# A hybrid decoder block on one Trainium2 core: the gate's row written in 128-byte pieces, and the two heads' A products untied

## The chip, the cores and the metric

The kernel runs on one core of a Trainium2 chip. The metric is the device time of one execution, in microseconds. Engines are named as in the profile: PE (TensorE's matmuls), PEld (its weight loads), DVE (VectorE), ACT (ScalarE), POOL (GpSimd) and SP (SyncE). All DMAs of the program are issued from SP's queue.

## The reference

A decoder block with two token mixers side by side on one normalised input, for 2048 tokens of width 1024:

```python
mod = einsum('bd,de->be', silu(c), ada_w) + ada_b
shift, scale, gate = split(mod, 3)
h = rmsnorm(x, norm_g) * (1 + scale) + shift
p = h @ w_in                                   # split into the branches' inputs
y_conv = conv_branch(...)                      # GLU, causal depthwise conv of 31, LayerNorm, swish, projection
y_rwkv = rwkv7_branch(...)                     # delta-rule state per head of 64, group norm, projection
m = sigmoid(g_conv) * y_conv + sigmoid(g_rwkv) * y_rwkv
out = rmsnorm(x + gate * (m @ w_out), final_g)
```

The RWKV branch runs a recurrence over tokens with one 64 by 64 state per head:

```python
sk = einsum('bhvk,bhk->bhv', state, kk_t)
state = state * w_t - sk * b_t + v_t * k_t     # outer products
o_t = einsum('bhvk,bhk->bhv', state, r_t)
```

The change touches two places of this: how `gate`, a vector of 1024 numbers, gets to DRAM, and the order in which one kind of small matrix product inside the RWKV branch is issued.

## The kernel before

The tokens are cut into 4 blocks of 512. In its first phase, up to about 2410 us, the kernel makes for each block all input projections, the convolution and the RWKV recurrence. In its second it makes the output projections, the final sum and the norm. All large products are made with operands split into a high and a low part, three matmuls for each (`mm3k`, line 207, tile `ps_main`). The weights' high and low parts are made once, kept in DRAM and loaded again for each later block by `load_w` (lines 183 and 184), as `w_hi` and `w_lo`, 512 KB each.

The RWKV branch works in chunks of 64 tokens, 8 chunks for a block. The 16 heads form 8 pairs, and two pairs form a group: 4 groups for each block. `pair` (line 457) prepares one pair of heads, both on the 128 partitions, head 0 on the first 64 and head 1 on the last 64. Its A products (line 535) multiply the tiles `BK` and `KR` of each chunk and head: matmuls with a contraction of 64 rows and 128 columns moving. They are made in two halves (`c4`) of 4 chunks. In each half, head 0 writes one PSUM tile of tag "aux" and head 1 another; VectorE then empties them with a mask into `Asb` (line 545). The tag has three buffers (`PAB`), which the pair's other small products use too, so the second half finds one buffer free, and needs another that VectorE has to empty first. Before the change, `tc.issue_after` ties the order: head 1's product of the first chunk is queued behind head 0's, and all products of the other three chunks of that half are queued behind head 1's first product. These ties are edges of order on TensorE alone, not waits.

A group's As blocks go to DRAM and back around a triangular inversion on POOL: `dA<-As` (line 619, 16 transfers of 16 KB), `La<-dA`, the loop of lines 631 to 636, `dT<-TT`, and `As<-dT` (line 646, 16 transfers of 16 KB).

The order on each engine comes from a planner: the program is traced in the order of the source, and when the context closes, a simulation of the engines takes the instructions by priority as their inputs and buffers come free in it. The engines then execute the order that it wrote, each its own queue in order. So while one group's small products wait, matmuls of line 207 for the convolution and the gates are put between them, and an edited order in one place can move others.

`gate` is made in block 1. `gate_cols` (line 870) is called after each of its four groups and makes two 128-number columns of the gate: it multiplies rows of `ada_w` by the activated `c` and sums them along the row on VectorE (line 878). After the last group, lines 881 to 883 finish the 128 by 8 tile `hgate_col`, and line 884 writes it to the DRAM vector `grow_d`, column by column. In block 2, `ogate` (line 149) reads parts of that vector, spread over all partitions (line 156), and multiplies the output weights by them. The write is issued at 1222.5 us of the span, the first read at 1395.4 us.

Of the kernel before, what the change touches and what calls it, by code (L numbers as in the profile page):

```python
# [9 lines left out]
F32 = mybir.dt.float32  # L10
# [8 lines left out]
P = 128  # L19
D = 1024  # L20
KT = D // P
# [61 lines left out]
def hybrid_block(ctx: ExitStack, tc: tile.TileContext, x, vecs, convk, w2a2, final_g, ada, w_in, w_co, w_ro, w_o, crow, out,  # L83
                 seq=2048, groups=(0, 1, 2, 3), phase2=True, dbg=None):
    nc = tc.nc
# [4 lines left out]
    cst = ctx.enter_context(tc.tile_pool(name="cst", bufs=1))  # L90
# [14 lines left out]
    grow_d = dp.tile([D], F32, name="grow_d", tag="grow_d")  # L105
# [7 lines left out]
    def vc(name, j=None):  # L113
        o, w = VOFF[name]
        return v[:, o:o + w] if j is None else v[:, o + j:o + j + 1]

    g_col = cst.tile([P, KT], F32, name="g_col")
    hgate_col = cst.tile([P, KT], F32, name="hgate_col")
    ghalf = cst.tile([P, 2, KT], F32, name="ghalf")
    shift_col = cst.tile([P, KT], F32, name="shift_col")  # L120
    ones = cst.tile([P, P], F32, name="ones")
# [12 lines left out]
    def flat(ap):  # L134
        return ap.rearrange("p a b -> p (a b)")
# [130 lines left out]
    nc.sync.dma_start(v, vecs)  # L266
    ab = vc("ada_b")
    hlg = cst.tile([P, KT], F32, name="hlg")
    hlb = cst.tile([P, 24], F32, name="hlb")[:, :KT]
    nc.vector.tensor_scalar(out=hlg, in0=vc("conv_ln_g"), scalar1=0.5, scalar2=None, op0=ALU.mult)  # L270
    nc.vector.tensor_scalar(out=hlb, in0=vc("conv_ln_b"), scalar1=0.5, scalar2=None, op0=ALU.mult)

# [57 lines left out]
    def hx(name):  # L330
        return xp.tile([P, TB], F32, name=name, tag="hx")
# [125 lines left out]
    def pair(b, q_, pr, h, lora, uv, Asb, rn, res):  # L457
# [30 lines left out]
        KR = l3.tile([P, NCH // 2, 4 * CH], F32, name="KR", tag="KR", bufs=KRB)  # L488
        BK = l3.tile([P, NCH // 2, 4 * CH], F32, name="BK", tag="BK", bufs=BKB)
# [14 lines left out]
        for c in range(NCH):  # L504
            nc.tensor.matmul(pss[prow(c % 2), c // 2, :], sq[:, c * CH:c * CH + CH], hones, start=True, stop=True,
                             skip_group_check=True)
# [20 lines left out]

        for c4 in range(NCH // 4):
            pA = [pa.tile([P, 2, 256], F32, name="aux", tag="aux") for _ in range(2)]

            def aprod(c, hh):
                cc, e = (c4 * 4 + c) // 2, c % 2
                es = slice(e * 128, e * 128 + 128)
                hs = slice(64 * hh, 64 * hh + 64)
                return nc.tensor.matmul(pA[hh][:, c // 2, es], BK[hs, cc, es], KR[hs, cc, es],  # L535
                                        start=(c == 0), stop=(c == 3), skip_group_check=True)

            with tc.issue_after(aprod(0, 0).ins):
                second = aprod(0, 1)
            with tc.issue_after(second.ins):  # L540
                for c in range(1, 4):
                    for hh in range(2):
                        aprod(c, hh)
            for hh in range(2):
                nc.vector.tensor_tensor(  # L545
                    out=Asb[:, hh, c4 * 4:c4 * 4 + 4, :].rearrange("p (a e) n -> p a (e n)", e=2),
                    in0=pA[hh], in1=flat(maskA).unsqueeze(1).broadcast_to([P, 2, 256]), op=ALU.mult)
# [24 lines left out]
        for c4 in range(NCH // 4):  # L572
            pt = pa.tile([P, 4, P], F32, name="aux", tag="aux")
            for c in range(4):
                cc, e = (c4 * 4 + c) // 2, c % 2
# [5 lines left out]
    def group(b, g, h, lora, fill):  # L581
        uv = l3.tile([P, NCH, 2, P], F32, name="uv", tag="uv", bufs=2)
        As = [l3.tile([P, 2, NCH, P], F32, name="As", tag="As", bufs=ASB) for _ in range(2)]
        R = [{}, {}]
        rn = lt.tile([P, 2, NCH // 2, 2], F32, name="rn", tag="rn")
        pairs = [pair(b, q, 2 * g + q, h, lora, uv, As[q], rn, R[q]) for q in range(2)]
        for i, q in enumerate(ORD):
            next(pairs[q])
# [281 lines left out]
    def gate_cols(g):  # L870
        for half in range(2):
            hs = slice(half * TB, half * TB + TB)
            sr = hx("sr")
            nc.sync.dma_start(sr, srow_d[hs].unsqueeze(0).broadcast_to([P, TB]))
            for k in (2 * g, 2 * g + 1):
                at = hx("gt")
                nc.sync.dma_start(at, ada[16 + k][:, hs])
                nc.vector.scalar_tensor_tensor(out=at, in0=at, scalar=1.0, in1=sr, op0=ALU.mult, op1=ALU.mult,
                                               accum_out=ghalf[:, half, k:k + 1])
        if g == 3:  # L880
            nc.vector.tensor_tensor(out=hgate_col, in0=ghalf[:, 0], in1=ghalf[:, 1], op=ALU.add)
            nc.vector.tensor_tensor(out=hgate_col, in0=hgate_col, in1=ab[:, 16:24], op=ALU.add)
            nc.vector.tensor_scalar(out=hgate_col, in0=hgate_col, scalar1=0.5, scalar2=None, op0=ALU.mult)
            nc.sync.dma_start(grow_d.rearrange("(n p) -> p n", p=P), hgate_col)

    mod = lt.tile([P, 16], F32, name="mod", tag="rn")

# [10 lines left out]
    for b in range(NB):  # L898
        h = hprep(b) if b else hprep0(x0, ada_steps())
        lora = lora_split(h)  # L900
        for g in groups:
# [32 lines left out]
            if b == 1:  # L934
                gate_cols(g)
# [136 lines left out]
    for b in range(NB):  # L1072
# [7 lines left out]
        for tt in range(NTT):  # L1080
            xh = []
            for half in range(2):
                n = 2 * tt + half
# [97 lines left out]
```

## Time and profile before

| | |
|---|---|
| median of 3 runs | 3003.95 us (2998.5 to 3004.62) |
| the profiled execution's own time | 3006.85 us |
| its span from the first instruction to the last | 3005.1 us |
| mean granted TensorE clock | 0.973 |
| instructions | 64777 |
| moved by DMA | 699.26 MB, mean 233 GB/s |

Times in the views are microseconds from the start of the span, durations of single instructions in ns where a view says so. In a timeline, a row gives start, length, engine, line, operation, output and inputs, and how many instructions were merged; in brackets stands how long the engine was idle before it, and what ended that. An fp32 matmul is recorded as two instructions, so 512 A products are 1024 records. A view by stretches gives for each engine its busy time and count, then the granted clock, the share of the DMA engines that was busy, and GB/s. In the DMA table the last number is the median from issue to landing.

### The profile page before, as it was taken

The numbers are of one execution on the slowest core, as the hardware profiler recorded it, in microseconds if no ns is written. First come the engines' busy times: TensorE is split into PE (matmuls) and PEld (weight loads), VectorE is DVE, ScalarE is ACT, GpSimd is POOL, SyncE is SP. The second block draws the span as 40 slices with busy tenths as digits, with TensorE's granted clock in tenths as the row PEclk, the third lists the DMA queues.
The fourth block names the chain that finished last, engine by engine and source line by source line (L and its number), as shares of the span: only waits on it lengthen the run. The fifth ranks groups of instructions, "written<-read, shape, count | busy, mean of one in ns | idle before, by whom it ended". The sixth has DMA issues, their size and how long they took to land.

```text
span 3005.1 us, 64777 instructions
## 1 busy us (share of the span) xinstructions
PE 2821.2 (94%) x25672; PEld 2649.1 (88%) x25672; DVE 2053.8 (68%) x3896; ACT 936.6 (31%) x1759; POOL 1251.2 (42%) x1786
## 2 busy tenths in 40 slices
PE   6889898999999999799999999999999998899998
PEld 5889798999899998799989988999989978688988
DVE  6687778787767676767676758776789634776433
ACT  4433334342324242323231413232333212333201
POOL 3555455535343435143434354626467104555000
PEclk9999999999999999899999999999999999999999
DMA  8666758664768588747575777655547678889674
GB/s 308 221 225 223 238 209 288 228 226 150 263 195 285 160 264 287 215 143 235 159 241 160 247 236 263 209 185 177 198 149 274 218 260 311 330 297 339 241 283 167
DMA packets 368674, 699.26 MB, mean 233 GB/s; under 512 B 136241, under 2 KB 154993, under 8 KB 368370
## 3 DMA queue, kind: packets, MB, share of 16 engines
q1 hardware_dynamic: 368370, 695.10, 68.5%
q8 instruction: 203, 3.33, 0.4%
q14 instruction: 101, 0.83, 0.1%
HBM read 506.14 MB, written 187.70 MB: 231 GB/s over the span
## 4 chain that ended last, share of the span: by engine, by line
PE 41%; DMA 14%; DVE 13%; POOL 11%; issue 4%; SPq 3%; ACT 2%; POOLq 0%; DVEq 0%; ACTq 0%
PE ps_main L207 30%; POOL TT L635 3%; POOL itmp L633 3%; DVE acc L782 3%; DMA w_st<-w_ro_t 2%; DMA w_gr<-grow_d 2%; DMA La<-dA 2%; PE aux L535 1%; PE xo L697 1%; DMA xt<-x_in 1%; DMA dT<-TT 1%; PE pout L1102 1%; PE pout L1103 1%; PE pout L1101 1%; PE xo L692 1%
## 5 line engine op out<-in xcount | busy, mean ns | idle before, releaser
L207 PE MATMUL ps_main<-h_hi,w_lo 128*128 128x256 f32 x4608 | 952.3, 285 | 23.8 <-DMA w_lo<-kl_in 14.9
L207 PE MATMUL ps_main<-h_hi,w_hi 128*128 128x256 f32 x4608 | 951.3, 285 | 14.2 <-ACT w_hi L190 5.4
L207 PE MATMUL ps_main<-h_lo,w_hi 128*128 128x256 f32 x4608 | 951.6, 285 | 0.3 <-DVE h_lo L364 0.3
L207 PEld LDWEIGHTS ps_main<-h_hi,w_lo 128*128 128x128 f32 x4608 | 719.2, 192 | 32.9 <-DMA w_lo<-kl_in 15.6
L207 PEld LDWEIGHTS ps_main<-h_hi,w_hi 128*128 128x128 f32 x4608 | 720.2, 192 | 26.4 <-ACT w_hi L190 6.3
L207 PEld LDWEIGHTS ps_main<-h_lo,w_hi 128*128 128x128 f32 x4608 | 719.5, 192 | 7.8 <-DVE h_lo L364 0.5
L782 DVE SCALAR_TENSOR_TENSOR acc<-u,ck,acc 128x512 f32<-128x512 f32 x928 | 697.9, 752 | 19.9
L633 POOL TENSOR_TENSOR itmp<-La,TT 128x126 f32<-128x126 f32 (+22 forms) x496 | 181.6, 366 | 158.6 <-DMA La<-dA 123.5
L635 POOL TENSOR_TENSOR TT<-TT,itmp 128x126 f32<-128x126 f32 (+22 forms) x496 | 189.7, 382 | 36.8
L689 ACT ACTIVATE Se<-S,pe 128x128 f32<-128x128 f32 x256 | 89.2, 396 | 258.9 <-DVE S L707 258.7
L192 POOL TENSOR_TENSOR w_lo<-w_st,w_hi 128x1024 fp32r<-128x1024 f32 x47 | 113.6, 2417 | 121.2 <-ACT w_hi L190 120.9
L707 DVE TENSOR_TENSOR S<-xo,Se 64x128 f32<-64x128 f32 x256 | 73.4, 287 | 101.3 <-PE xo L703 98.3
L190 ACT CAST w_hi<-w_st 128x1024 fp32r<-128x1024 f32 x71 | 74.6, 1051 | 178.8 <-DMA w_st<-w_in_t 133.1
L699 DVE TENSOR_TENSOR uv<-xo,rn 64x256 f32<-64x256 f32 x128 | 53.8, 420 | 94.8 <-PE xo L697 93.6
L694 DVE TENSOR_TENSOR XO<-xo,XO 128x256 f32<-128x256 f32 x128 | 53.8, 420 | 81.9 <-PE xo L692 67.7
L570 POOL TENSOR_TENSOR BK<-BK,pe 128x1024 f32<-128x1024 f32 x32 | 62.1, 1941 | 113.7 <-PE aux L535 82.3
L794 ACT ACTIVATE th<-ps_main 128x512 f32<-128x512 f32 x64 | 38.2, 597 | 196.7 <-PE ps_main L207 162.9
L692 PE MATMUL xo<-S,KR 128*128 128x128 f32 x512 | 84.7, 289 | 15.7 <-DVE S L707 15.6
L545 DVE TENSOR_TENSOR As<-aux,maskA 128x512 f32<-128x512 f32 x128 | 83.0, 685 | 24.0 <-PE aux L535 23.1
L535 PE MATMUL aux<-KR,BK 64*128 64x128 f32 x1024 | 95.1, 303 | 4.1 <-POOL KR L523 2.5
L697 PE MATMUL xo<-XO,As 64*64 64x64 f32 x1024 | 90.7, 228 | 8.4 <-DVE XO L694 8.2
L697 PEld LDWEIGHTS xo<-XO,As 64*64 64x64 f32 x1024 | 71.2, 136 | 29.3 <-DVE XO L694 10.8
(301 smaller groups left out, 5290.4 us busy)
## 6 DMA issues: line engine op xcount, KB each, us to landing
w_hi<-kh_in SPq DMA_DIRECT2D x219, 512.0 KB, 5.4
w_lo<-kl_in SPq DMA_DIRECT2D x219, 512.0 KB, 4.1
w_st<-w_in_t SPq DMA_DIRECT2D x73, 512.0 KB, 4.7
kh_in<-w_hi SPq DMA_DIRECT2D x71, 512.0 KB, 2.9
kl_in<-w_lo SPq DMA_DIRECT2D x71, 512.0 KB, 3.7
w_hi<-kh_ro SPq DMA_DIRECT2D x32, 512.0 KB, 6.3
w_lo<-kl_ro SPq DMA_DIRECT2D x32, 512.0 KB, 5.7
w_hi<-kh_co SPq DMA_DIRECT2D x32, 512.0 KB, 5.9
```

What stands on the lines that cost most here:

```text
L190: nc.scalar.copy(hi, st)
L192: lo_eng.tensor_tensor(out=lo, in0=st, in1=hi.bitcast(F32), op=ALU.subtract)
L207: nc.tensor.matmul(ps[:, qs], ww[:, k, :], aa[k][:, qs], start=(k == 0 and t == 0 and q == 0), stop=(k == KT - 1 and t == 2 and q == ms - ...
L535: return nc.tensor.matmul(pA[hh][:, c // 2, es], BK[hs, cc, es], KR[hs, cc, es], start=(c == 0), stop=(c == 3), skip_group_check=True)
L545: nc.vector.tensor_tensor(out=Asb[:, hh, c4 * 4:c4 * 4 + 4, :].rearrange("p (a e) n -> p a (e n)", e=2), in0=pA[hh], in1=flat(maskA).unsqu ...
L633: nc.gpsimd.tensor_tensor(out=tmp[:, :ni, :nt], in0=La[:, j:j + 1, j + 1:].broadcast_to([P, ni, nt]), in1=TT[:, :ni, j:j + 1].broadcast_to ...
L635: nc.gpsimd.tensor_tensor(out=TT[:, :ni, j + 1:], in0=TT[:, :ni, j + 1:], in1=tmp[:, :ni, :nt], op=ALU.add)
L689: nc.scalar.mul(Se[:, q, :], Sg[:, q, :], R[q]["pe"][:, c:c + 1])
L692: nc.tensor.matmul(xo[:, q, :], R[q]["KR"][:, cc, es], Sg[:, q, :], start=(q == 0), stop=(q == 1), skip_group_check=True)
L697: nc.tensor.matmul(xo[pr_, q, hs], As[q][pr_, hh, c, kcol(e)], XO[pr_, c, q, hs], start=(q == 0 and hh == 0), stop=(q == 1 and hh == 1), s ...
L707: nc.vector.tensor_tensor(out=Sg[hs, :, hs], in0=xo[hs, 2:4, hs], in1=Se[hs, :, hs], op=ALU.add)
L782: nc.vector.scalar_tensor_tensor(out=acc if i + 1 < HALO else yj, in0=u[:, i:i + TB], scalar=ck[:, j, i:i + 1], in1=acc, op0=ALU.mult, op1 ...
```

## The change

Three edits. The gate's tile `hgate_col` becomes a part of a larger tile of two 32-column planes, cleared at the start. After the column is finished, VectorE transposes the first plane into the second in blocks of 32 by 32, so that the numbers that lie one behind the other in DRAM lie along a partition in runs of 32. Four DMAs then write 8 runs of 128 bytes each, in place of one DMA that writes 1024 single numbers. The padding of another small tile, `hlb`, goes from 24 to 32 columns. And the A products lose their ties: the same products are traced in the same order, chunk by chunk and head by head, without the edges.

```diff
-    hgate_col = cst.tile([P, KT], F32, name="hgate_col")
+    g32 = cst.tile([P, 2, 32], F32, name="g32")
+    nc.vector.memset(g32, 0.0)
+    hgate_col = g32[:, 0, 0:KT]
...
-    hlb = cst.tile([P, 24], F32, name="hlb")[:, :KT]
+    hlb = cst.tile([P, 32], F32, name="hlb")[:, :KT]
...
             pA = [pa.tile([P, 2, 256], F32, name="aux", tag="aux") for _ in range(2)]
-
-            def aprod(c, hh):
+            for c in range(4):
                 cc, e = (c4 * 4 + c) // 2, c % 2
                 es = slice(e * 128, e * 128 + 128)
-                hs = slice(64 * hh, 64 * hh + 64)
-                return nc.tensor.matmul(pA[hh][:, c // 2, es], BK[hs, cc, es], KR[hs, cc, es],
-                                        start=(c == 0), stop=(c == 3), skip_group_check=True)
-
-            with tc.issue_after(aprod(0, 0).ins):
-                second = aprod(0, 1)
-            with tc.issue_after(second.ins):
-                for c in range(1, 4):
-                    for hh in range(2):
-                        aprod(c, hh)
+                for hh in range(2):
+                    hs = slice(64 * hh, 64 * hh + 64)
+                    nc.tensor.matmul(pA[hh][:, c // 2, es], BK[hs, cc, es], KR[hs, cc, es],
+                                     start=(c == 0), stop=(c == 3), skip_group_check=True)
...
             nc.vector.tensor_scalar(out=hgate_col, in0=hgate_col, scalar1=0.5, scalar2=None, op0=ALU.mult)
-            nc.sync.dma_start(grow_d.rearrange("(n p) -> p n", p=P), hgate_col)
+            nc.vector.transpose(g32[:, 1, :], g32[:, 0, :])
+            for i in range(4):
+                nc.sync.dma_start(grow_d.rearrange("(n i t) -> i n t", i=4, t=32)[i], g32[32 * i:32 * i + KT, 1, :])
```

## The prediction

> **What bounds the kernel now.** I read the page first: the busy shares, then the chain that ended last.
>
> ```profile
> PE 2821.2 (94%) x25672; PEld 2649.1 (88%) x25672; DVE 2053.8 (68%) x3896; ACT 936.6 (31%) x1759; POOL 1251.2 (42%) x1786
> ...
> PE 41%; DMA 14%; DVE 13%; POOL 11%; issue 4%; SPq 3%; ACT 2%; POOLq 0%; DVEq 0%; ACTq 0%
> ```
>
> TensorE is occupied for 94% of the span. Its share of the chain is only 41%, so other things do end waits, but each of them briefly. Next I asked for the busy time by stretches: once for the whole mixer phase, 85 to 2410 us, in which all A products lie, and once closely around the gate's row.
>
> ```profile
> core 0: us, PE busy (x) PEld busy (x) DVE busy (x) ACT busy (x) POOL busy (x), PEclk, DMA share, GB/s
> 85.00:2410.00 2325.00, 2206.57 (x21996) 2109.94 (x21995) 1689.89 (x3112) 749.49 (x1379) 1057.52 (x1635) 0.97 0.66 218
> ```
>
> TensorE has work in 2206.57 of 2325 us, 95%, so 118 us are idle. Work added to TensorE here mostly lengthens the kernel.
>
> ```profile
> 1220.00:1224.00 4.00, 4.00 (x36) 3.96 (x35) 3.38 (x11) 0.00 (x0) 0.00 (x0) 1.00 0.30 31
> 1224.00:1228.00 4.00, 0.16 (x2) 0.00 (x0) 4.00 (x11) 0.00 (x0) 0.00 (x0) 0.86 1.49 84
> 1228.00:1232.00 4.00, 0.00 (x0) 0.00 (x0) 0.41 (x1) 0.00 (x0) 0.00 (x0) 0.50 0.49 31
> 1232.00:1236.00 4.00, 0.00 (x0) 0.00 (x0) 0.00 (x0) 0.60 (x1) 0.00 (x0) 0.50 0.61 114
> ```
>
> From 1228 to 1236 no engine has more than a few tenths of a microsecond of work: the program stands still. The timelines of SyncE's queue and of TensorE show what it waits for.
>
> ```profile
> 1212.24 10.16 SPq L646 DMA_DIRECT2D As<-dT  x16
> 1222.49 0.38 SPq L884 DMA_DIRECT2D grow_d<-hgate_col  x1
> 1222.92 0.58 SPq L765 DMA_DIRECT2D ro_d<-th  x1
> 1223.60 0.39 SPq L184 DMA_DIRECT2D w_lo<-kl_in  x1
> ```
> ```profile
> 1223.77 0.39 PE L207 MATMUL ps_main<-h_lo,w_hi 128*128 128x256 f32 x2
> 1236.99 0.79 PE L207 MATMUL ps_main<-h_hi,w_lo 128*128 128x256 f32 x2 [12.83 <-DMA w_lo<-kl_in]
> ```
>
> The gate's row (L884) is issued at 1222.49. The low half of the next weight tile is issued 1.1 us behind it, and TensorE stands for 12.83 us until that lands. The DMA table of the page and the view of line 884 give the two durations to compare.
>
> ```profile
> w_lo<-kl_in SPq DMA_DIRECT2D x219, 512.0 KB, 4.1
> ```
> ```profile
> L884 SPq DMA_DIRECT2D grow_d<-hgate_col x1: 382/382/382, 1222.5 to 1222.5; - x1
> ...
> DMA to landing us min/median/max: 10.9/10.9/10.9
> ```
>
> A transfer like the late one needs 4.1 us at the median. The gate's row carries 4 KB, but as 8 columns by 128 partitions, hence 1024 pieces of 4 bytes, and needs 10.9 us. What is issued behind it inherits that.
>
> **Part 1: the gate's row.** Removed: one transfer of 1024 pieces. Added: a transpose on VectorE, four transfers of 8 pieces of 128 bytes, and a memset at the start. The nearest row for the new transfers is the one that writes As to DRAM, also in runs of 32 floats, 128 bytes (16 KB each, so 128 pieces); for the transpose, line 661.
>
> ```profile
> L619 SPq DMA_DIRECT2D dA<-As x256: 302/430/1792, 96.9 to 2282.1; - x128
> ...
> DMA to landing us min/median/max: 1.4/1.7/7.5
> ```
> ```profile
> L661 DVE STREAM_TRANSPOSE T<-As x128: 255/299/305, 175.8 to 2348.6; 32x128 f32<-32x128 f32 x128
> ```
> ```profile
> 1216.90 0.16 DVE L883 TENSOR_SCALAR hgate_col<-hgate_col 128x8 f32<-128x8 f32 x1
> ```
>
> The transpose costs about 0.3 us after 1217.06. SyncE reaches the row at 1222.49, so 5 us of cover remain; without it, the 0.3 us would fall on SyncE's queue. The wait that the first new transfer has on the transpose is therefore over before SyncE comes to it; behind it in the queue stand the ro_d store and the weights. The memset is of the size of the others at the start:
>
> ```profile
> 0.91 0.17 DVE L122 MEMSET ones<- 128x128 f32 x1 [0.91 <-PEq L1174]
> ...
> 4.92 0.20 DVE L300 COPY maskA<-m 64x64 f32<-64x64 f32 x1 [0.92 <-POOL m L297]
> ```
>
> It disappears in the 0.92 us that VectorE waits there anyway; without that cover it would be 0.17 us. The larger tiles move what is allocated behind them by 256 bytes; no row prices an address, and I count nothing for it.
>
> Three more issues at 0.43 us move the weight's issue from 1223.60 to 1224.9; at the rate of the sixteen issues above (10.16/16 = 0.635) to 1225.5. Its landing then takes 4.1 us, because the queues are nearly empty (31 GB/s in 1220 to 1224), so TensorE resumes at 1229.0 instead of 1236.99: 8.0 us saved. With 3.5 us of landing the saving is 8.6. The other bound is the median of the same transfers in the crowded surroundings:
>
> ```profile
> w_lo<-kl_in SPq DMA_DIRECT2D x8, 512.0 KB, 6.8
> ```
>
> With 6.8 us and the late issue it is 1232.3, a saving of 4.7. I take 7.5, near the empty-queue end. As every engine stands still here, all of it counts. What is late next is the same weight, for about 5 us instead of 12.8, now because sixteen small transfers stand ahead of it on SyncE.
>
> A rule speaks against this part: the Trainium skill, "DMA: Bandwidth & Descriptors", section "Rules for kernel authors", wants many small transfers made into one, since under 64 KB one mostly pays overhead. By that rule four transfers are worse than one; the trace has the one at 10.9 us and small ones at 1.7, overlapping at an issue each 0.43. It is the fourth case below.
>
> **Part 2: the A products.** Each half of a pair has 4 chunks by 2 heads, 8 products of 64 rows, recorded as 16 instructions. Heads 0 and 1 lie in different halves of the array. What is at stake is whether they run beside each other.
>
> ```profile
> 398.74:399.74 1.00, 1.00 (x17) 1.00 (x17) 1.00 0.47 184
> ```
> ```profile
> 410.37 1.03 PE L576 MATMUL aux<-ident,BK 128*128 128x128 f32 x8
> 411.16 0.48 PE L207 MATMUL ps_main<-h_hi,w_lo 128*128 128x256 f32 x2
> ```
>
> The first is the view of line 535 in one microsecond: 16 instructions (and one overlapping) with heads alternating. The nearest row for a single head is the transposes, also 128 columns of fp32: 8 in 0.79 us to the next start. So a half costs 1.0 us in pairs and 2 x 0.79 = 1.58 with each head alone.
>
> ```profile
> 1130.63 1.38 PE L535 MATMUL aux<-KR,BK 64*128 64x128 f32 x18
> 1131.93 0.38 PE L207 MATMUL ps_main<-h_hi,w_lo 128*128 128x256 f32 x1
> ...
> 1135.40 0.72 PE L535 MATMUL aux<-KR,BK 64*128 64x128 f32 x8
> 1136.05 0.71 PE L703 MATMUL xo<-uv,tk 128*128 128x128 f32 x4
> 1136.69 0.71 PE L535 MATMUL aux<-KR,BK 64*128 64x128 f32 x6
> 1137.33 0.39 PE L207 MATMUL ps_main<-h_hi,w_hi 128*128 128x256 f32 x1
> ```
>
> Here is one pair's order: 18 instructions are the first half plus the lone first product of the second half, and the other 14 follow 3.5 us later. That product of head 0 finds the third "aux" buffer; head 1 has to wait until VectorE has emptied one. The tie holds chunks 1 to 3 of head 0 back until then. Without it, nothing holds them: the planner, which let the first product run at once, will let the next three follow, alone, and head 1 comes later, alone. First halves have both buffers and mostly stay in pairs.
>
> A second half costs now 0.2 (lone product, a quarter of 0.79) + 0.9 (14 in pairs) + 0.1 of re-entry = 1.2 us, an estimate from these rows; cut in two as shown it is 0.2 + 0.65 + 0.64 = 1.49. Alone it is 1.58. So +0.38 against the clean form, +0.1 against the cut one, and +0.58 if compared with a whole half in pairs. Times 32 second halves (4 blocks x 4 groups x 2 pairs): 12, 3 or 19 us. I take 12, since the order will be cut as often as today. By the idle share above I let 0.8 of it pass: 10 us. VectorE gets head 0 sooner:
>
> ```profile
>   PE aux L535: 23.1, 24
> ```
>
> It waited 23.1 us in 24 times for these products; at its 13% of the chain that is worth 3 us if all goes, and I take 1. A gain beyond that is excluded as long as TensorE has other matmuls in hand, which it has. Part 2: +9 us.
>
> The Trainium skill, "TensorEngine Tiling (Array Packing)", section "Theoretical Speedup", allows up to 2x where the contraction is 64 or less; by that rule a lone half would take 2.0 us, the second halves +0.8 each, 25.6 us in all, and with 0.8 of it passed on the time would be 3016, an estimate that falls in with the slower case below. The trace's 1.58 speaks for less.
>
> **The sum** against the profiled execution (span 3005.1, its time 3006.85): 3006.85 - 7.5 + 9 = 3008.35. The median of the three runs shown, 3003.95, lies 2.9 lower: 3005.5.
>
> **The rivals.**
> *Heads stay in pairs, or their price isn't felt.* The planner might put the same order down without the tie, or fill idle slots with the lone products: then only the gate's saving stays, 3003.95 - 7.5 = 2996.5. For it: 118 us of idle time exist in the phase. Against it: the 18-instruction rows show head 0 going ahead whenever it may. An untied source with an unchanged order is also the case in which part 2 does nothing.
> *Lone heads at the full price (slower).* At 0.58 us for each of the 32 second halves and nothing hidden, 18.6 us; less 7.5, that is 3015. It decides from 13.5 us of lost TensorE time upward (7.5 + 6). For it: 95% busy. Against it: today's second halves are already partly lone.
> *Four fixed costs.* If each of the four transfers had to land before the next moves, three more times 1.7 = 5.1 us in place of the 1.3 counted: the saving falls by 3.8 to 3.7, and the time is 3009.3. Against it: landings overlap in the small transfers of today.
>
> **How the numbers follow.** A measurement of this kernel tells about 0.2%, 6 us, from no change (the three runs spread 2998.5 to 3004.62). Forecast 0.41, pairs kept 0.28, full price 0.22, four costs 0.09. The forecast's own range is 2997 to 3012: part 1 between 4.7 and 8.6, part 2 between 3 and 15 us. Faster (below 2998): 0.24 of pairs kept and 0.06 of the forecast, 0.30. Slower (above 3010): 0.20 of full price, 0.08 of the forecast, 0.04 of four costs, 0.32. The rest, 0.38, within. The range reaches from 2994, under the pairs-kept time, to 3017, over the full-price time.
>
> **What would show it.** Right: L884 four times with landings near 2 us, the wait for w_lo there shorter than 6 us, rows of L535 with about 24 instead of 18 instructions, second halves in two lone runs of 8, L535's busy sum above the 95.1 us of this row:
>
> ```profile
> L535 PE MATMUL aux<-KR,BK 64*128 64x128 f32 x1024 | 95.1, 303 | 4.1 <-POOL KR L523 2.5
> ```
>
> Wrong: 18-instruction rows as before (then faster), a stall of 10 us or more near 1224 (part 1 failed), or new stalls elsewhere from a changed order, which no row of before prices.

## The result, and the profile after

| | before | after |
|---|---|---|
| median, measured side by side | 3004.47 us (2997.87 to 3015.95, 10 runs) | 3021.18 us (3008.53 to 3029.11, 10 runs) |
| the profiled execution's own time | 3006.85 us | 3018.02 us |
| its span | 3005.1 us | 3016.3 us |
| mean granted clock | 0.973 | 0.972 |

The medians lie 16.7 us apart. The ratio of the two kernels is 1.0042, with a 95% interval from 1.0023 to 1.0060: by it the change makes the kernel slower by about 13 us. The forecast was 3005.5, and the end of its range 3017.

From the page of after, the busy line and the chain:

```profile
PE 2846.3 (94%) x25672; PEld 2675.5 (89%) x25672; DVE 2055.9 (68%) x3898; ACT 933.4 (31%) x1759; POOL 1249.9 (41%) x1786
...
PE 49%; DMA 17%; DVE 13%; POOL 10%; issue 4%; SPq 4%; ACT 3%; POOLq 0%; ACTq 0%; DVEq 0%
```

TensorE is busy for 25.1 us more. 20.9 of them are in the A products, whose group had 95.1 us. The group of after, then three rows of TensorE's timeline:

```profile
L537 PE MATMUL aux<-KR,BK 64*128 64x128 f32 x1024 | 116.0, 299 | 3.9 <-POOL KR L525 3.5
```
```profile
389.89 2.05 PE L537 MATMUL aux<-KR,BK 64*128 64x128 f32 x24
391.87 0.51 PE L209 MATMUL ps_main<-h_lo,w_hi 128*128 128x256 f32 x2
...
394.30 1.16 PE L537 MATMUL aux<-KR,BK 64*128 64x128 f32 x8
395.38 0.38 PE L209 MATMUL ps_main<-h_hi,w_lo 128*128 128x256 f32 x1
```

The first row is a half in pairs and then head 0's four products of the second half, alone: 24 instructions where 18 stood. Head 1's follow alone, 8 instructions. Up to the next start, 24 take 1.98 us and 8 take 1.08. So this part came as forecast, only dearer: a lone run of 8 costs 0.98 us (1.98 less the 1.0 of a half in pairs) to 1.08 us, and not 0.79.

The gate's row did not come as forecast. These are SyncE's queue, TensorE's wait and the view of the tile `grow_d` in after:

```profile
1223.81 0.38 SPq L186 DMA_DIRECT2D w_lo<-kl_in  x1
...
1227.23 0.59 SPq L186 DMA_DIRECT2D w_lo<-kl_in  x1
...
1236.26 2.15 SPq L881 DMA_DIRECT2D grow_d<-g  x4
```
```profile
1227.77 0.80 PE L209 MATMUL ps_main<-h_hi,w_lo 128*128 128x256 f32 x2 [2.92 <-DMA w_lo<-kl_in]
```
```profile
L881 SPq DMA_DIRECT2D grow_d<-g x4: 263/272/295, 1236.3 to 1238.2; - x4
```

The view names no landing for the four. In the trace their semaphores were last raised 3.3 to 4.5 us after each issue.

The stall of 12.83 us is gone. But the weight that TensorE waits for is no longer behind the row: the row has moved 14 us back, behind three loads of `w_lo`. That is not the work of the 32 pieces. It is the order, as e2 below shows.

### The profile page after: what moved, and what is told of

Same layout as the page of the kernel before. It is cut to its first block, busy times and chain, and to the rows that moved or that the text cites. A ratio compares the mean times of both kernels' runs of the same rounds, so it can differ in the third digit from the quotient of the medians.

```text
span 3016.3 us, 64745 instructions
## 1 busy us (share of the span) xinstructions
PE 2846.3 (94%) x25672; PEld 2675.5 (89%) x25672; DVE 2055.9 (68%) x3898; ACT 933.4 (31%) x1759; POOL 1249.9 (41%) x1786
## 3 DMA queue, kind: packets, MB, share of 16 engines
q1 hardware_dynamic: 367394, 695.10, 67.9%
## 4 chain that ended last, share of the span: by engine, by line
PE 49%; DMA 17%; DVE 13%; POOL 10%; issue 4%; SPq 4%; ACT 3%; POOLq 0%; ACTq 0%; DVEq 0%
PE ps_main L209 36%; POOL TT L630 3%; POOL itmp L628 2%; DVE acc L777 2%; DMA w_st<-w_ro_t 2%; DMA w_st<-w_in_t 2%; DMA w_st<-w_co_t 2%; PE aux L537 2%; DMA w_gr<-grow_d 2%; PE xo L692 1%; SPq L641 1%; PE pout L1100 1%; PE pout L1098 1%; PE pout L1099 1%; PE xo L698 1%
## 5 line engine op out<-in xcount | busy, mean ns | idle before, releaser
L209 PE MATMUL ps_main<-h_hi,w_lo 128*128 128x256 f32 x4608 | 948.5, 285 | 11.3 <-DMA w_lo<-kl_in 7.9
L537 PE MATMUL aux<-KR,BK 64*128 64x128 f32 x1024 | 116.0, 299 | 3.9 <-POOL KR L525 3.5
L537 PEld LDWEIGHTS aux<-KR,BK 64*128 64x128 f32 x1024 | 99.4, 200 | 14.4 <-POOL KR L525 4.5
L540 DVE TENSOR_TENSOR As<-aux,maskA 128x512 f32<-128x512 f32 x128 | 83.6, 685 | 26.8 <-PE aux L537 25.8
L434 ACT ACTIVATE t<-ps_main,mu 128x512 f32<-128x512 f32 x96 | 65.6, 684 | 102.5 <-PE ps_main L209 95.5
```

The costliest lines, as they stand in the source:

```text
L209: nc.tensor.matmul(ps[:, qs], ww[:, k, :], aa[k][:, qs], start=(k == 0 and t == 0 and q == 0), stop=(k == KT - 1 and t == 2 and q == ms - ...
L434: nc.scalar.activation(t1, ps, AF.Identity, scale=mu1[:, mi:mi + 1])
L540: nc.vector.tensor_tensor(out=Asb[:, hh, c4 * 4:c4 * 4 + 4, :].rearrange("p (a e) n -> p a (e n)", e=2), in0=pA[hh], in1=flat(maskA).unsqu ...
```

## The experiments

Each was measured beside the kernel before on the same chip; ratios are to before, with 95% intervals. Where orders are compared, the kernels' instructions were laid side by side on each engine, numbers of buffers left out.

### One part at a time

First theory: the loss is the TensorE time of the heads that now run alone ("lone heads"), passed on nearly whole. Its rival: the order that the planner writes.

**e1_gate_only**: after, with the old ties of the A products.

```
+            with tc.issue_after(aprod(0, 0).ins):
+                second = aprod(0, 1)
+            with tc.issue_after(second.ins):
...
```

> The gate's row in 32 pieces as in the change, the A products tied as before. Theory (the lost time is TensorE time of heads that run alone; the gate's edit by itself saves): the A products' busy sum stays at 95 us (within 2), the wait for w_lo near 1224 us is under 6 us instead of 12.83, the time is 6 to 10 us under the kernel before, ratio 0.997 to 0.998. Rival A (the four transfers or the moved addresses cost the time): as slow as the changed kernel, ratio 1.003 to 1.005. Rival B (any new order of the planner loses): anything, but with new stalls and the busy sum of the A products unchanged.

0.9971 (0.9952 to 0.9991). The row stands ahead of the weight as in before, and the wait is 4.64 us instead of 12.83; SyncE's queue and TensorE of this kernel:

```profile
1220.75 1.29 SPq L888 DMA_DIRECT2D grow_d<-g  x4
...
1223.00 0.40 SPq L186 DMA_DIRECT2D w_lo<-kl_in  x1
```
```profile
1227.68 0.80 PE L209 MATMUL ps_main<-h_hi,w_lo 128*128 128x256 f32 x2 [4.64 <-DMA w_lo<-kl_in]
```

Part 1 by itself saves 8.7 us (the forecast had 7.5). The wait is 8.2 us shorter; the rest can be order, since TensorE's order in this kernel differs from before's, mostly between about 1240 and 1560 us.

**e2_untied_only**: before, with the A products of after.

```
-            with tc.issue_after(aprod(0, 0).ins):
...
+                for hh in range(2):
+                    hs = slice(64 * hh, 64 * hh + 64)
+                    nc.tensor.matmul(pA[hh][:, c // 2, es], ...)
```

> The A products untied as in the change, the gate's row in one transfer of 1024 pieces as before. Theory: A products' busy sum 115 to 117 us, a wait of 10 us or more behind the gate's row remains, time 14 to 21 us over the kernel before, ratio 1.005 to 1.007, so slower than the changed kernel by what the gate's edit saves. Rival A: the untying is free, ratio 0.999 to 1.001.

0.9995 (0.9975 to 1.0016), with A products at 117.1 us. With 22 us of added work the time is that of before. The old row of 1024 pieces no longer stalls TensorE either:

```profile
1236.02 0.39 SPq L184 DMA_DIRECT2D w_lo<-kl_in  x1
...
1242.87 0.37 SPq L877 DMA_DIRECT2D grow_d<-hgate_col  x1
```
```profile
1236.82 0.80 PE L207 MATMUL ps_main<-h_hi,w_lo 128*128 128x256 f32 x2 [2.81 <-DMA w_lo<-kl_in]
...
1255.74 0.47 PE L207 MATMUL ps_main<-h_hi,w_hi 128*128 128x256 f32 x2 [0.61 <-DMA w_hi<-kh_in]
...
1257.23 0.50 PE L207 MATMUL ps_main<-h_hi,w_lo 128*128 128x256 f32 x2 [0.78 <-DMA w_lo<-kl_in]
```

In the untied order the planner puts the row behind the loads by itself. The row still needs 11.3 us to land, but TensorE's waits for the weights behind it are short, 0.61 and 0.78 us. So this kernel has lost the gate's stall without part 1, and its result is not the price of the heads alone.

**e3_heads_alone**: after, with the two loops exchanged, so that in every half head 0's four products stand ahead of head 1's.

```
-            for c in range(4):
+            for hh in range(2):
...
+                for c in range(4):
```

> The changed kernel with the two loops of the A products exchanged: all four chunks of head 0 first, then all of head 1, so that the first halves run alone as well. Theory: each first half goes from 1.0 us to about 2.0 us, the A products' busy sum rises by another 25 to 35 us over the changed kernel's 116.0, the time by 18 to 32 us over the changed kernel, ratio to before 1.010 to 1.015. Rival B (the loss is a less lucky order, not the products): about the changed kernel's time, 1.004, whatever the busy sum.

0.9966 (0.9942 to 0.9989), with still more work in the A products (122.4 us). That is 6.4 us over after, not the 25 to 35 expected. A first half and the lone head 0 behind it, in TensorE's timeline of this kernel:

```profile
244.67 2.26 PE L537 MATMUL aux<-KR,BK 64*128 64x128 f32 x24
246.86 0.39 PE L209 MATMUL ps_main<-h_hi,w_hi 128*128 128x256 f32 x1
```

They take 2.19 us to the next start, against 1.98 in after; three lone runs of 0.98 would be 2.94. So the heads still ran partly beside each other where one follows the other. The first theory fell all the same: more time in the A products than in after, and a faster kernel than before. (Its order differs from after's from the first block on.)

**e4_tile_only**: before with the larger tile and padding; order as before but for the memset.

```
+    g32 = cst.tile([P, 2, 32], F32, name="g32")
+    nc.vector.memset(g32, 0.0)
+    hgate_col = g32[:, 0, 0:KT]
```

> Only the larger, cleared tile and the wider padding: the addresses behind move by 256 bytes and VectorE has one more memset; the gate's row goes in 1024 pieces as before, the A products are tied. Theory: the time of before within 0.2%, the wait of 12 to 13 us for w_lo is still there. Rival A (moved addresses): slower by 0.3% or more.

0.9988 (0.9968 to 1.0008): addresses cost nothing in the tied order.

So each part alone is harmless or good, and only together, as in after, they lose.

### Other orders

**e5_same_order** repeats after's order exactly, with the four transfers in reverse.

```
-            for i in range(4):
+            for i in (3, 2, 1, 0):
```

> The changed kernel with its four transfers issued in the opposite order; every engine has the same order of instructions as the changed kernel. New theory, after the first four runs: untying costs some 20 us of TensorE time, most of which comes back as shorter waits; the gate's edit saves only where the row stands ahead of a needed weight tile, which the untied order does not have; the rest of the changed kernel's loss, some 14 us, is the order that the planner made behind the gate's row, from 1234 us on. It expects the changed kernel's time again, ratio 1.003 to 1.006, low clock and waits in blocks 3 and 4 as there. Rival C (the changed kernel's ratio was chance of the chip it was timed on): 0.998 to 1.002, like the untied kernel without the gate's edit.

1.0039 (1.0020 to 1.0058): it is the order or the contents, not chance.

**e6_untied_later**, **e7_untied_1024_later** and **e8_tied_later** are after, e2 and e1 with the row's transfers written down at the start of block 2.

```
+            if b == 2 and g == 0:
+                for i in range(4):
+                    nc.sync.dma_start(grow_d.rearrange(...)[i], g32[32 * i:32 * i + KT, 1, :])
```

> The changed kernel (untied, 32 pieces) with the four transfers traced at the start of block 2 instead of the end of block 1: the same work, another order behind that place. New theory: A products' busy sum 114 to 118 us as in the changed kernel, but the time is that of a new order, 0.996 to 1.002. Rival D (untied products and four transfers are slow together in any order): 1.003 to 1.006.

> Untied, one transfer of 1024 pieces, traced at the start of block 2. New theory: busy sum of the A products 114 to 118 us, time 0.997 to 1.003, higher if the row stands ahead of a weight tile (a wait for w_lo of 10 us or more, then over 1.001). Rival D: as the untied kernel without the gate's edit, 0.998 to 1.001, since without the four transfers there is nothing to lose.

> Tied, 32 pieces, the four transfers traced at the start of block 2. New theory: A products' busy sum 90 to 95 us, no long wait behind the gate's row, time 0.994 to 1.000 with the order's scatter. Rival E (orders do not scatter, each edit has its own fixed price): the time of the tied kernel with the gate's edit, 0.996 to 0.998.

1.0072 (1.0049 to 1.0095, four runs), 1.0011 (0.9994 to 1.0029) and 0.9965 (0.9946 to 0.9984). In e6 the order is a new one, and the worst. In e7 it stayed e2's, only the row itself moved. e8 is before's order but for some tens of neighbours near the row; its four transfers stand behind two loads of `w_lo`, so they are both cheap and out of the way, and it gains 10.5 us. It, e1 and e3 beat both kernels.

**e9_after_nudge**, **e10_untied_nudge**, **e11_after_nudge2** and **e12_before_nudge** add one memset of a dead tile to after (twice, at different places), e2 and before, to make the planner draw anew.

```
+            if b == 2 and g == 0:
+                nc.gpsimd.memset(ghalf, 0.0)
```

> The changed kernel with one tiny GpSimd memset (128 by 16, of a tile that is dead by then) traced at the start of block 2, which changes the planner's order on all engines from there on, and nothing of the work. Order theory (the changed kernel's loss beyond the untying is one unlucky order from 1234 us on): a time drawn anew, most likely between 0.998 and 1.004, busy sum of the A products 114 to 118 us. Rival D (untied products together with the four transfers are slow in any order; three of three kernels so far): 1.003 to 1.007.

> The untied kernel with one transfer of 1024 pieces, with the same memset. Order theory: drawn anew around the same middle as the changed kernel with the memset, 0.998 to 1.004. Rival D: stays at 0.998 to 1.001.

> The changed kernel with the same memset one group later in block 2: its order is the changed kernel's until there, another one after. Order theory: 0.998 to 1.004, another value than the other nudged kernel. Rival D: 1.003 to 1.007.

> The kernel before (tied, 1024 pieces) with the same memset at the start of block 2. It shows how far a new order alone moves the time. Order theory: a shift of a few tenths of a per cent either way, 0.997 to 1.003, the wait of 12 to 13 us behind the gate's row unchanged, since it lies before the changed order. Rival D: within 0.1% of before.

1.0018 (0.9997 to 1.0039), 0.9999 (0.9985 to 1.0014), 1.0042 (1.0026 to 1.0059, four runs) and 1.0000 (0.9985 to 1.0015). As a lottery they failed: laid side by side, each has its model's order but for the memset, whatever was expected of them. They are repeats. What they left standing was a rival: an untied kernel with four short transfers is slow in any order.

### Order, addresses and pieces crossed

Order, the 256-byte shift of later tiles, and the pieces still went together. **e13_untied_tile** has e2's order and pieces at after's addresses (e2 with e4's edit). **e14_after_old_place** has after's order and pieces at the old addresses:

```
+    gx = late.enter_context(tc.tile_pool(name="gx", bufs=1))
+    g32 = gx.tile([P, 2, 32], F32, name="g32")
```

**e16_after_4bytes** has after's order, and 1024 pieces again; **e17_untied_128** has e2's order and 128 pieces of 32 bytes (it leaves out the right order of the gate's numbers in DRAM, so its output is another one):

```
+                nc.sync.dma_start(grow_d.rearrange("(n i t) -> i t n", i=4, t=32)[i], hgate_col[32 * i:32 * i + 32])
```
```
+            nc.sync.dma_start(grow_d.rearrange("(p n) -> p n", n=KT), hgate_col)
```

> The heads untied and the row in 1024 pieces as in the second experiment, but with after's tile and padding, so that every later tile lies 256 bytes per partition further on, as in after. The order on every engine is that of the second experiment, to the instruction, besides one memset. Order theory (the order that the planner wrote behind 1234 us for after is the slow one; addresses and pieces cost nothing): 0.999 to 1.002, as the three kernels with this order had (0.9995, 1.0011, 0.9999). Address theory (untied and at after's addresses is slow): 1.002 to 1.006, as the four with after's order had (1.0042, 1.0039, 1.0018, 1.0042).

> After, its order on every engine to the instruction, with the two-plane tile in a pool of its own above the early pools, so that every constant, weight and working tile below it lies where it lay before the change. Order theory: 1.002 to 1.006, as after. Address theory: 0.999 to 1.002. Transfer theory (four transfers of 128-byte pieces in an untied kernel are slow): 1.002 to 1.006 as well.

> After, its order on every engine to the instruction, but each of the four transfers writes its 256 numbers one by one from the untransposed plane: 1024 pieces of 4 bytes again. Order theory: 1.002 to 1.006, as after, since the row stands behind the weights that are next needed and its reader comes 150 us later. Transfer theory (128-byte pieces in an untied kernel are what is slow): 0.999 to 1.002. Pieces priced as in the prediction and not hidden: 7.5 us more than after, 1.006 or more.

> The second experiment, its order on every engine to the instruction, but its one transfer writes 128 pieces of 32 bytes: the row gets to DRAM in the order of the partitions, so the gate's numbers are permuted in the output. Order theory: 0.999 to 1.002. Transfer theory (what is slow in an untied kernel is a short write of the row): 1.002 to 1.006. If a shorter write gains in this order what it gained in the tied one: 0.996 to 0.998.

| order | kernel | addresses | row | ratio (95%) |
|---|---|---|---|---|
| after's | after | new | 32 pieces | 1.0042 (1.0023 to 1.0060) |
| after's | e14 | old | 32 | 1.0024 (1.0008 to 1.0040) |
| after's | e16 | new | 1024 | 1.0058 (1.0035 to 1.0081) |
| e2's | e2 | old | 1024 | 0.9995 (0.9975 to 1.0016) |
| e2's | e13 | new | 1024 | 0.9989 (0.9973 to 1.0004) |
| e2's | e17 | old | 128 | 0.9992 (0.9978 to 1.0006) |

The order decides. With e5, e9 and e11, six kernels have after's order: 1.0018 to 1.0058, mean 1.0037. With e7 and e10, five have e2's: 0.9989 to 1.0011, mean 0.9997. Neither addresses nor pieces move a kernel from one group to the other; both rivals fell. A smaller price of the pieces in after's order is not excluded: e16 is the slowest of its six, with a wide interval. As e13 and after differ only in the gate's row, and the orders are equal up to it (SyncE's to about 1234 us, TensorE's to 1246), it is what the planner wrote behind that place that costs 0.4%, or 12 us.

### Where in the order, and what the pieces are worth

The eleven profiles can be averaged by order, and then show what one alone can't. The blocks end with their last A product.

| mean of profiles | block 1 | block 2 | block 3 | block 4 | rest | span | idle | TensorE work | lost to half clock |
|---|---|---|---|---|---|---|---|---|---|
| before's order (before, e4, e12) | 550.5 | 584.4 | 598.8 | 533.2 | 734.2 | 3001.0 | 182.3 | 2758.4 | 60.4 |
| e2's order (5) | 559.9 | 593.1 | 589.0 | 525.3 | 736.0 | 3003.4 | 157.0 | 2778.4 | 67.9 |
| after's order (6) | 558.2 | 594.3 | 588.2 | 532.3 | 738.7 | 3011.7 | 165.3 | 2773.8 | 72.6 |

(Lost to half clock is half of TensorE's busy time at a granted clock of 0.5; work is the rest of its busy time. Work differs by some us between the last two though the matmuls are the same, so it is known to no better than that.) Of the 8.3 us between the last two rows 7.0 lie in block 4, and of these 5.9 in one stretch, A products 832 to 864, 1897 to 2013 us in the mean of the six: 116.0 us (113.2 to 117.8) against 110.1 (110.0 to 110.5). 3.0 of the 5.9 are idle time of TensorE, 1.6 are lost to half clock, 1.3 are work. SyncE's queue and TensorE there, in after, and then SyncE's queue in e2:

```profile
1946.59 0.38 SPq L185 DMA_DIRECT2D w_hi<-kh_in  x1
1947.49 10.10 SPq L641 DMA_DIRECT2D As<-dT  x16
1957.69 0.38 SPq L790 DMA_DIRECT2D gc_d<-th  x1
1958.17 0.38 SPq L186 DMA_DIRECT2D w_lo<-kl_in  x1
```
```profile
1963.32 0.79 PE L209 MATMUL ps_main<-h_hi,w_lo 128*128 128x256 f32 x2 [4.99 <-DMA w_lo<-kl_in]
```
```profile
1936.92 0.32 SPq L184 DMA_DIRECT2D w_lo<-kl_in  x1
...
1945.66 9.35 SPq L639 DMA_DIRECT2D As<-dT  x16
```

In after a load of `w_lo` stands behind the 16 issues of `As<-dT`, and TensorE waits 5.0 us for it (2.8 to 5.0 in the six). In e2 one more load, at 1936.92, went ahead, and there is no such wait. In four of the six, after among them, the clock is then granted at half:

```profile
core 0: us, PE busy (x) PEld busy (x) DVE busy (x) ACT busy (x) POOL busy (x), PEclk, DMA share, GB/s
...
1960.00:1964.00 4.00, 0.68 (x3) 0.69 (x4) 3.67 (x12) 0.00 (x0) 2.26 (x3) 0.68 0.97 294
1964.00:1968.00 4.00, 4.00 (x21) 4.00 (x21) 3.78 (x5) 0.00 (x0) 0.00 (x0) 0.50 1.03 416
```

**e18_as_from_act** issues those 16 transfers from ScalarE's queue.

```
-                        nc.sync.dma_start(As[q][sl, hh, e::2, sl], ...)
+                        (nc.scalar if (b, g) == (3, 0) else nc.sync).dma_start(As[q][sl, hh, e::2, sl], ...)
```

> After, with the 16 transfers As<-dT of the last block's first group issued from ScalarE's queue and not from SyncE's. The order is after's up to that place (about 1870 us) on every engine, and on SyncE behind it too but for a few neighbours; on TensorE, VectorE and ScalarE some tens of instructions change places behind it. In the six profiles with after's order the stretch between A products 832 and 864 of the 1024 (1897 to 2013 us) takes 116.0 us and holds a wait of 5.0 us for a w_lo that stands behind these 16 issues (10.1 us of SyncE's queue); in the five with the other order it takes 110.1. Theory that this queue place is what the order of after costs: the wait at 1958 us is gone, the stretch takes 109 to 112 us, and the ratio falls from the mean of the six (1.0037) to 1.001 to 1.0025. Rival (the wait is one of many, and a time saved there is given back at the next one): 1.003 to 1.005, the stretch of the next pairs longer.

1.0050 (1.0033 to 1.0068), and 118.7 us for the stretch. The wait for `w_lo` is gone, and another has its place; ScalarE and TensorE of this kernel:

```profile
1941.92 5.24 ACTq L641 DMA_DIRECT2D As<-dT  x9
1947.20 0.60 ACT L789 ACTIVATE th<-ps_main 128x512 f32<-128x512 f32 x1 [5.24 <-DMA As<-dT]
```
```profile
1947.85 0.80 PE L209 MATMUL ps_main<-h_hi,w_hi 128*128 128x256 f32 x2 [6.22 <-ACT th L789]
```

Now the `th` that empties TensorE's PSUM tile stands behind the issues. That the issues cause the wait is shown, since it follows them from queue to queue. What the kernel would gain without it stays open: this edit only moved it, and the ratio is the one that its rival (a time saved there is given back at the next wait) had named.

**e15_alone_1024** is e3 with the old tile and row; some tens of instructions around 1250 us change places.

> The third experiment (both heads' products alone in every half) with the old tile and the row in 1024 pieces. The order is the third experiment's besides some tens of instructions around 1250 us. In that one the row is issued at 1220.1 us, ahead of a w_lo at 1223.3 that TensorE needs next, as in the kernel before and not as in after. Theory (what the 1024 pieces cost hangs on whether a needed weight stands behind the row): a wait of 8 to 13 us for w_lo near 1230 us again, and a ratio of 0.9985 to 1.0, 6 to 9 us above the third experiment's 0.9966. Rival (in an untied kernel the pieces cost nothing anywhere, and the third experiment's gain is its heads' order alone): 0.9955 to 0.9975, no such wait.

0.9999 (0.9982 to 1.0015), 3.3 thousandths above e3. The ratio is as the theory had it, the wait is not: 0.41 us for `w_lo`, and 5.5 for something else. SyncE, ScalarE, VectorE, TensorE, and the busy time in two stretches:

```profile
1224.78 0.32 SPq L788 DMA_DIRECT2D gr_d<-th  x1
1225.44 0.37 SPq L877 DMA_DIRECT2D grow_d<-hgate_col  x1
```
```profile
1238.75 0.60 ACT L755 ACTIVATE th<-ps_main 128x512 f32<-128x512 f32 x1 [8.37 <-DMA gr_d<-th]
```
```profile
1239.38 0.69 DVE L757 SCALAR_TENSOR_TENSOR th<-th,ps_main 128x512 f32<-128x512 f32 x1 [5.56 <-ACT th L755]
```
```profile
1240.12 0.79 PE L207 MATMUL ps_main<-h_hi,w_hi 128*128 128x256 f32 x2 [5.51 <-DVE th L757]
```
```profile
1230.00:1234.00 4.00, 4.00 (x35) 4.00 (x36) 3.82 (x8) 0.38 (x1) 0.00 (x0) 1.00 1.40 161
1234.00:1238.00 4.00, 0.61 (x6) 0.41 (x4) 0.00 (x0) 0.00 (x0) 0.00 (x0) 1.00 0.88 74
```

Of the 1265 packets that start in the first stretch 1063 are shorter than 512 bytes: that is the row. In the second the DMA engines are busy for 88% and move 74 GB/s; few short packets start there any more, but the large ones are slow. A store issued 0.66 us ahead of the row lands 13.9 us later (6.9 in e3), ScalarE waits for its buffer, VectorE for ScalarE, and TensorE for VectorE. From the profile, e15's and e3's TensorE wait 6.9 and 2.5 us between 1220 and 1250. So about 4 of the 10 us that the ratios show are found; the two profiles differ by more than that before the row, where the orders are the same (6.6 us at the end of block 2).

This kernel also answers the first theory once more. Against the profile of before, its TensorE is busy for 30.5 us longer (2851.7 against 2821.2), its idle time is 152.6 us against 184.0, and its time is the same.

## Why the prediction was wrong

**What bounds the kernel.** Right in its rows, too strong in its reading. "Work added to TensorE here mostly lengthens the kernel" does not hold: in e2's order and in e15, 20 to 30 us of added work were made up for by less idle time, of which the gate's stall is only a part.

**Part 1** was right by itself (8.7 us in e1 for 7.5, the next wait 4.6 us for the 5 named; 10.5 in e8, where the row also moved). By their semaphores in e1's trace each of the four transfers landed 1.2 us after its issue, and the whole row 2.2 us after the first: the 1.7 was near, the four overlap, and the fixed costs did not add up. Addresses cost nothing that e4 or e13 could show.

**Part 2, the price.** The mechanism came as described: pairs first, then two lone runs of 8, rows of 24. The term "+0.38" was mis-sized. The A products' busy sum went from 95.1 to 116.0 us, 0.65 for each of 32 second halves. The row of `L576` transposes was a poor stand-in. The rule of the Trainium skill ("TensorEngine Tiling (Array Packing)", "Theoretical Speedup") that the prediction weighed and set aside was the nearer one: it allows up to 2x, and a half with each head alone takes 0.98 + 1.08 = 2.06 us against 1.0 in pairs.

**Part 2, "I let 0.8 of it pass".** Wrong in the other direction. In e2's order the work is 20.0 us up, the idle time 25.3 down (some 10 of it the gate's stall) and the clock's loss 7.5 up: 2.2 us in all. VectorE did not gain its 1 us: its wait for A products went from 23.1 to 25.8 in after. A price of the heads by itself is not to be had from the runs. Against the tied kernels without the stall (e1 and e8, 0.9968 in the mean), e2's order is 0.29%, 8.7 us, slower, which is near the "+9", and after is 21 us slower than e1, as much as the whole added TensorE time. But e3, untied too and with more time in the A products, is as fast as e1. The price comes with the order.

**The sum is the step that failed.** "-7.5" and "+9" were added as if the order around them stayed as it was, and a changed order had no term. First, once untied, the row is queued behind the weights that TensorE needs next: the stall goes whatever the pieces (e2 waits 2.81 us with 1024 pieces, after 2.92 with 32), and there is nothing left for shorter pieces to save (in e2's order e17's shorter row gains nothing). In that order, untying and lost stall together come to 0.9997, 1 us less than before. The sum had 1.5 us more; that it is so near is luck, since the stall went by another way than part 1's. Second, what the shorter row then does is to change the order behind it, and that order is 0.4%, 12 us, slower than e2's. These 12 of the 13 us are the order's, a term that the sum put at nothing.

**The rivals.** "Full price (slower)" had the sign and 3015 us, but not the cause. "Heads stay in pairs" and "four fixed costs" did not happen. The time, 3021.18, lay beyond the end of the range. The prediction's last words named what happened, "new stalls elsewhere from a changed order, which no row of before prices", as a thing that would prove it wrong. It should have been a rival with a chance and a width: the three untied orders that part behind about 1234 us lie at 0.9997 (five kernels), 1.0037 (six) and 1.0072 (e6).

**What stays open.** About half of after's loss is placed: 5.9 us in the stretch around the 16 issues, of 8.3 in the profiles and 12 in the ratios. Of the rest the profiles show 2.7 us in the last phase (738.7 against 736.0 us), where profiles of one order lie 7 to 8 us apart, and it is not traced to a wait. Nor is it shown why the planner's two orders differ in this way.

## What to carry to other kernels

Where a planner writes the order, two edits don't add: measure each alone and both together before summing. A small scattered transfer costs what is queued beside it, so look at its neighbours on the queue, not at its length. And to tell an order from an edit, build kernels that have the one without the other, and compare their orders with buffer numbers left out.

## What the runs showed of the hardware

**The clock.** In all 20 profiles the granted clock changes in windows of 3.41 us. A window in which TensorE was idle for 2.0 us or more in all was followed by one at half clock in 425 of 425 cases; with 1.0 to 1.25 us idle in 45 of 199; with under 0.25 us in 180 of 15197. So a wait of 2 us can cost another 1.7 us of work, half of such a window. The Trainium skill, "TensorE: Matmul & The Clock Gate", "HAM oscillation — how this bites in real kernels", gives the rule of no idle gaps over about 3.4 us; here 2 us within a window were enough, and the measurement decides.

**Pieces of 4 bytes.** 1024 of them in one transfer take 10.3 to 11.4 us to land in six profiles (10.9 in before, 11.3 in e2) and 14.6 in e15; 128 pieces of 32 bytes take 5.9 (e17), four transfers of 8 by 128 bytes 2.2 in all (e1). The small pieces come with a slow stretch for what is beside them: in e15 a store issued just ahead of the row took 13.9 us, and 6.9 in e3 with its 32 pieces.
